# Three of the four weight block sums of each dual of the short convolution's projection by adding transfers, gate loads on SyncE's queue

## The chip, the core and the metric

One core of a Trainium2 chip runs the whole program. The metric is the device time of one execution in microseconds (us); a profile is one further execution taken by the hardware profiler. The engines are TensorE (PE, with weight loads as PEld), VectorE (DVE), ScalarE (ACT), GpSimd (POOL) and SyncE (SP). SP, ACT and POOL also issue DMA transfers, each from a queue of its own that is worked in order.

## What is computed

One layer of a streaming encoder, on 1024 rows of 1024 channels, in float32. The part that matters here is the short convolution's branch of the merge:

```python
h = rms_norm(x, norm_mix_g[l]) * (1.0 + sc1) + sh1
proj = jnp.einsum('bsd,de->bse', h, w_in[l])
b_s, c_s, v_s, v_c, gl_c, gate_br = jnp.split(proj, SPLITS[:-1], axis=-1)
y_a = b_s * causal_dwconv(c_s * v_s, conv_short_w[l])
y_a = jnp.einsum('bsc,cd->bsd', y_a, w_short_out[l])
...
g_a, g_b = jnp.split(jax.nn.sigmoid(gate_br), 2, axis=-1)
mix = jnp.einsum('bsd,de->bse', g_a * y_a + g_b * y_b, w_o[l])
```

The change is in the projection by `w_short_out` and in the loading of `g_a`.

## The kernel before

Channels lie on the 128 partitions and time on the free axis, in two halves of 512 columns. Each float32 operand of a matmul is split into a high part and a low part, so one product of tiles is three matmuls: high by high (line 397), weight high by input low (398), weight low by input high (400). A weight tile of 128 x 1024 is loaded on SP's queue (`load`, line 218), its high part `wh` is cast by ACT (234) and its low part `wl` subtracted by DVE, or by POOL for some (235). `wh` and `wl` have three buffers each; the raw tiles have five, three in one pool and two in another, taken in turn by `raw_tile`.

Most projections are done as duals: two rows of output blocks by a fast scheme of seven block products in place of eight, in the order 1, 2, 6, 5, 7, 3, 4 (`PRODUCTS`). The weights of the products are blocks 11, 12, 21, 22 of the dual or sums of them:

- product 1 uses 11, product 2 uses 12, product 4 uses 22;
- product 5 uses s1 = 21 + 22;
- product 6 uses s2 = 11 + s1;
- product 7 uses 21 + 11;
- product 3 uses 12 + s2.

`apart_units` makes these weights: it loads each block just ahead of its use and adds on the engine it is given. For the short convolution's projection it is called with VectorE for both duals (line 353), so a dual has seven loads (11, 12, 21, 22, 11, 12, 22) and four sums (line 312), of which s2 goes to a tile of its own.

`plan` lists the weights in the order of use, and `next_w` keeps them two products ahead of the matmuls. For this stage the order `ya_order` is product 1 of both duals, product 2 of both, then 6, 5, 7, 3, 4 of dual 0 and the same of dual 1. A product is 24 matmuls. Tile's scheduler lists the instructions of every engine and queue once, at build time, from dependencies and from the orders given with `issue_after`; at run time each engine and queue works its list in order, and waits where an operand or a buffer isn't ready.

`ya_evac` takes the banks of a product. Its `out` (line 1088) loads half of a gate row `ga` (128 x 512, 256 KB) from DRAM on POOL's queue, and DVE multiplies it with the bank into `ma` (lines 747 and 751). Gate tiles share a pool of six buffers with the squares and the statistics of the layer norm, which runs beside this stage: DVE subtracts the mean (1015), ACT squares (1017), DVE sums the squares (1021). The convolved rows `cv` are loaded on SP's queue (1013). Behind the stage follow the other branch's projection (`yb`), whose weights come from `in_w_conf` on the same queue, and on POOL's queue the loads of the other gate (line 1144). Ahead of it POOL subtracts the last low parts of the input projection and adds up `tot` (993).

Of the kernel before, what the change touches and what calls it, by code (L numbers as in the profile page):

```python
# [38 lines left out]
ALU = mybir.AluOpType  # L39
# [76 lines left out]
PRODUCTS = "1265734"  # L116
# [15 lines left out]
def block_kernel(ctx: ExitStack, tc: tile.TileContext, x0, xT, c, vecs, ada, w_first, w_plain, w_duals,  # L132
                 w_short, w_conf, w_o, w_fi, w_fo0, w_fo1, outT):
    nc = tc.nc
# [30 lines left out]
    def ps2_tile(name):  # L165
        return ps2p.tile([P, H], F32, tag="ps2", name=name)
# [4 lines left out]
    def s_tile(name, dt=F32):  # L171
        return hl_tile(name, dt)

    def g_tile(name):
        return gsp.tile([P, H], F32, tag="gs", name=name)

    def f32(t):
        return t.bitcast(F32)

    halves = (slice(0, H), slice(H, T))  # L180
# [28 lines left out]
    def raw_tile(n=1024, home=None):  # L209

        if home is None:
            raws.append(raws.pop(0))
        return (home or raws[-1]).tile([P, 1024], F32, tag="raw", name="raw")[:, :n]

    def load(src, n=1024, home=None):
        raw = raw_tile(n, home)
        with tc.issue_after(x1_load[0]) if x1_load else ExitStack():
            load.ins = nc.sync.dma_start(raw, src).ins
        return raw
# [8 lines left out]
    def split_w(raw, n, after=(), lo_engine=nc.vector):  # L228
        wh = whp.tile([P, 1024], F32R, tag="wh", name="wh")[:, :n]
        wl = wlp.tile([P, 1024], F32R, tag="wl", name="wl")[:, :n]  # L230
        with ExitStack() as order:
            for ins in after:
                order.enter_context(tc.issue_after(ins))
            hi = nc.scalar.copy(wh, raw)  # L234
            lo = lo_engine.tensor_tensor(wl, raw, f32(wh), ALU.subtract)  # L235
        split_w.hi, split_w.lo = hi.ins, lo.ins
        if n == T and lo_engine is nc.gpsimd:
            pool_los.append((hi.ins, lo.ins))
        return wh, wl
# [66 lines left out]
    def apart_units(mats, eng, on_eng=PRODUCTS, after=None):  # L306


        a = {}

        def add(out, x, y):
            unit.eng.tensor_tensor(out, x, y, ALU.add)  # L312
            return out

        def get(b):
            return load(mats[("11", "12", "21", "22").index(b)])

        def unit(m):
            unit.eng = eng if m in on_eng else nc.gpsimd
            if m in "12":  # L320
                raw = get("1" + m)
            elif m == "6":
                for b in ("21", "22", "11"):
                    a[b] = get(b)
                with tc.issue_after(after()) if after else ExitStack():
                    a["s1"] = add(a["22"], a["21"], a["22"])
                    if "6" in on_eng:
                        raw = a["s2"] = add(raw_tile(), a["11"], a["s1"])
                    else:
                        a["s3"] = add(a["21"], a["21"], a["11"])  # L330
                        raw = a["s2"] = add(a["11"], a["11"], a["s1"])
            elif m == "7":
                raw = a["s3"] if "s3" in a else add(a["21"], a["21"], a["11"])
            elif m == "3":
                raw = get("12")
                add(raw, raw, a["s2"])
            else:
                raw = a["s1"] if m == "5" else get("22")
            return split_w(raw, 1024, (), unit.eng)

        return {m: (lambda m=m: unit(m)) for m in PRODUCTS}

    plan = [None] * KC
    plan += [(w_plain[0], 1024)]
    n_duals = len(PAIRS) // 2
# [4 lines left out]
    win_order += [(d, m) for d in range(BEGUN + 1, n_duals) for m in PRODUCTS]  # L350
    plan += [win_units[d][m] for d, m in win_order]
    ya_order = [(d, m) for m in "12" for d in range(2)] + [(d, m) for d in range(2) for m in PRODUCTS[2:]]
    ya_units = [apart_units([w_short[d, m] for m in range(4)], nc.vector) for d in range(2)]
    plan += [ya_units[d][m] for d, m in ya_order]
    plan += [(w[k], 1024) for w in (w_conf, w_o) for ks in (range(KC), SECOND[KEPT:]) for k in ks]
    ready = []
# [212 lines left out]
    gate_dram = {(b, j): dram.tile([P, T], F32, name=f"gate_{b}{j}") for b in "ab" for j in range(KC)}  # L569
# [173 lines left out]
    def plus(out, ps, b):  # L743
        plus.ins = nc.vector.tensor_tensor(out, ps, b, ALU.add).ins
# [150 lines left out]
    b = {}  # L895
# [185 lines left out]
    def ya_evac(d, banks):  # L1081

        st = {}

        def out(i, row, h, op, ps):
            j = 4 * d + 2 * i + row
            ga = g_tile("ga")
            nc.gpsimd.dma_start(ga, gate_dram["a", j][:, halves[h]])
            ma[j, h] = s_tile(f"ma{j}{h}")
            op(ma[j, h], ps, ga)  # L1090
            ma["ins"] = plus.ins

        def evac(i, m, ps):
            if m == "1":
                if d == 1:
                    banks["y", i] = ps2_tile("y")
                nc.scalar.copy(banks["y", i], ps)
            elif m in "65":
                st[m, i] = s_tile("vz")
                nc.scalar.copy(st[m, i], ps)  # L1100
            elif m == "2":
                out(i, 0, 0, times, ps)
            elif m == "7":
                z = ps2_tile("z")
                plus(z, ps, st["5", i])
                out(i, 1, 1, minus_times, z)
            elif m == "3":
                plus(ps, ps, st["6", i])
                out(i, 0, 1, times, ps)
            else:  # L1110
                out(i, 1, 0, minus_times, ps)
        return evac
# [577 lines left out]
```

## Time and profile before

| | us |
|---|---|
| three runs, median (lowest to highest) | 1460.13 (1459.64 to 1461.17) |
| the profiled execution | 1462.66 |
| its span, first to last instruction | 1460.9 |
| PE busy, of the span | 1448.1 |
| DVE busy | 1188.5 |
| ACT busy | 627.2 |
| POOL busy | 516.3 |

The granted TensorE clock was 0.999. A row of a timeline gives the start in us, the busy time in us, the engine, the line of the kernel, the operation, output and inputs by name, and how many instructions were merged; in square brackets stands how long the engine was idle before and what ended it. A row of groups gives count, busy us, mean ns, and the idle time before with its releasers. SPq and POOLq are the queues from which DMA is issued. A PE row's duration overlaps its neighbours, since matmuls are pipelined: the distance of two starts is what one costs.

### The profile page before, as it was taken

The numbers are of one execution on the slowest core, as the hardware profiler recorded it, in microseconds if no ns is written. First come the engines' busy times: TensorE is split into PE (matmuls) and PEld (weight loads), VectorE is DVE, ScalarE is ACT, GpSimd is POOL, SyncE is SP. The second block draws the span as 40 slices with busy tenths as digits, with TensorE's granted clock in tenths as the row PEclk, the third lists the DMA queues.
The fourth block names the chain that finished last, engine by engine and source line by source line (L and its number), as shares of the span: only waits on it lengthen the run. The fifth ranks groups of instructions, "written<-read, shape, count | busy, mean of one in ns | idle before, by whom it ended". The sixth has DMA issues, their size and how long they took to land.

```text
span 1460.9 us, 17711 instructions
## 1 busy us (share of the span) xinstructions
PE 1448.1 (99%) x6394; PEld 1187.8 (81%) x6394; DVE 1188.5 (81%) x1634; ACT 627.2 (43%) x911; POOL 516.3 (35%) x484
## 2 busy tenths in 40 slices
PE   9999999999999999999999999999999999999997
PEld 4878888888888888788888888888888888888887
DVE  7897999987988979999787698777777666866676
ACT  4773333333333346465235465444444443322235
POOL 0007777677677761111021001111111005662505
PEclk9999999999999999999999999999999999999999
DMA  9542222323222357476685436655554449996903
GB/s 351 206 139 85 73 94 79 116 73 101 72 87 73 123 201 281 130 233 206 209 293 203 152 101 216 214 178 198 169 177 148 143 148 327 395 392 193 359 1 116
DMA packets 88522, 257.68 MB, mean 176 GB/s; under 512 B 10177, under 2 KB 12865, under 8 KB 88434
## 3 DMA queue, kind: packets, MB, share of 16 engines
q1 hardware_dynamic: 43792, 142.04, 29.1%
q0 software_dynamic: 40608, 101.92, 21.2%
q10 hardware_dynamic: 4034, 12.59, 2.4%
q8 instruction: 50, 0.82, 0.2%
q14 instruction: 38, 0.31, 0.1%
HBM read 190.97 MB, written 65.54 MB: 176 GB/s over the span
## 4 chain that ended last, share of the span: by engine, by line
PE 88%; issue 4%; DVE 3%; POOL 2%; DMA 1%; ACT 1%; POOLq 0%; DVEq 0%; ACTq 0%
PE bank L400 11%; PE bank L397 11%; PE bank L398 11%; PE x L400 8%; PE x L398 8%; PE x L397 8%; PE z L397 3%; PE z L398 3%; PE z L400 3%; PE mix L400 2%; PE mix L397 2%; PE yb L400 2%; PE yb L397 2%; PE mix L398 2%; PE yb L398 2%
## 5 line engine op out<-in xcount | busy, mean ns | idle before, releaser
L234 ACT CAST wh<-raw 128x1024 fp32r<-128x1024 f32 (+3 forms) x255 | 260.9, 1026 | 475.5 <-PE bank L398 149.5
L235 DVE TENSOR_TENSOR wl<-raw,wh 128x1024 fp32r<-128x1024 f32 (+3 forms) x176 | 209.1, 1190 | 49.3 <-ACT wh L234 46.6
L235 POOL TENSOR_TENSOR wl<-raw,wh 128x1024 fp32r<-128x1024 f32 x79 | 191.4, 2426 | 105.4 <-ACT wh L234 105.3
L972 DVE SCALAR_TENSOR_TENSOR c<-diff,vec,c 128x512 f32<-128x512 f32 x232 | 168.4, 752 | 2.7
L1331 POOL DMA_DIRECT2D hid<-stage x70 | 37.3, 533 | 343.9 <-DVE stage L438 332.5
L400 PE MATMUL bank<-th,wl 128*128 128x512 f32 x312 | 121.5, 389 | 0.4 <-POOL wl L235 0.4
L398 PE MATMUL bank<-tl,wh 128*128 128x512 f32 x312 | 121.4, 389 | 0.0
L397 PE MATMUL bank<-th,wh 128*128 128x512 f32 x312 | 121.4, 389 | 0.0
L972 DVE SCALAR_TENSOR_TENSOR c<-u,wsum,c 128x512 f32<-128x512 f32 x112 | 84.4, 753 | 2.3
L400 PEld LDWEIGHTS bank<-th,wl 128*128 128x128 f32 x312 | 58.6, 188 | 13.0 <-POOL wl L235 0.8
L398 PEld LDWEIGHTS bank<-tl,wh 128*128 128x128 f32 x312 | 58.6, 188 | 12.2
L398 PE MATMUL x<-tl,wh 128*128 128x512 f32 x176 | 68.5, 389 | 0.0
L397 PE MATMUL x<-th,wh 128*128 128x512 f32 x176 | 68.5, 389 | 0.0
L400 PE MATMUL x<-th,wl 128*128 128x512 f32 x176 | 68.4, 390 | 0.0
L397 PEld LDWEIGHTS bank<-th,wh 128*128 128x128 f32 x312 | 58.6, 188 | 12.1
L437 ACT CAST stage<-g 128x512 fp32r<-128x512 f32 x60 | 37.3, 621 | 68.0 <-DMA hid<-stage 42.9
L438 DVE TENSOR_TENSOR stage<-g,stage 128x512 fp32r<-128x512 f32 x60 | 41.3, 690 | 27.2 <-ACT stage L437 27.1
L1355 POOL DMA_DIRECT2D th<-hid x77 | 41.2, 535 | 53.5 <-PE x L400 23.4
L312 POOL TENSOR_TENSOR raw<-raw 128x1024 f32<-128x1024 f32 x8 | 20.5, 2567 | 110.0 <-ACT th L437 104.9
L400 PE MATMUL yb<-zsh,wl 128*128 128x512 f32 x128 | 49.8, 389 | 0.0
L397 PE MATMUL yb<-zsh,wh 128*128 128x512 f32 x128 | 49.8, 389 | 0.0
L398 PE MATMUL yb<-zsl,wh 128*128 128x512 f32 x128 | 49.8, 389 | 0.0
(829 smaller groups left out, 4135.4 us busy)
## 6 DMA issues: line engine op xcount, KB each, us to landing
hid<-stage POOLq DMA_DIRECT2D x70, 512.0 KB, 4.7
raw<-in_w_duals SPq DMA_DIRECT2D x57, 512.0 KB, 3.5
raw<-in_w_fi SPq DMA_DIRECT2D x54, 512.0 KB, 4.7
th<-hid POOLq DMA_DIRECT2D x77, 256.0 KB, 6.0
tl<-hid POOLq DMA_DIRECT2D x77, 256.0 KB, 6.1
ada<-in_ada SPq DMA_DIRECT2D x24, 512.0 KB, 5.7
raw<-in_ada SPq DMA_DIRECT2D x24, 512.0 KB, 4.9
raw<-in_w_fo SPq DMA_DIRECT2D x16, 512.0 KB, 6.1
```

Of the source, the lines that this page charges most:

```text
L234: hi = nc.scalar.copy(wh, raw)
L235: lo = lo_engine.tensor_tensor(wl, raw, f32(wh), ALU.subtract)
L312: unit.eng.tensor_tensor(out, x, y, ALU.add)
L397: nc.tensor.matmul(ps, wh, xh, start=first, stop=False, skip_group_check=again)
L398: nc.tensor.matmul(ps, wh, xl, start=False, stop=False, skip_group_check=again)
L400: mm3.ins = nc.tensor.matmul(ps, wl, xh, start=False, stop=last, skip_group_check=again).ins
L437: t_split.act = nc.scalar.copy(hi, src).ins
L438: t_split.ins = nc.vector.tensor_tensor(lo, src, f32(hi), ALU.subtract).ins
L972: tap.ins = nc.vector.scalar_tensor_tensor(out=out, in0=src[:, s : s + H], scalar=wt, in1=acc, op0=ALU.mult, op1=ALU.add).ins
L1331: nc.gpsimd.dma_start(hid_dram[key], s)
L1355: nc.gpsimd.dma_start(t, hid_dram[key][:, s])
```

## The change

A new function `added_units` makes the weights of the two duals of this stage in place of `apart_units`. Block 22 is loaded and 21 is added onto it by a transfer that adds (s1); 11 is loaded and DVE adds s1 to it (s2); 21 is loaded and 11 is added onto it by a transfer (product 7); 12 is added by a transfer onto s2 in its own tile, once product 6's parts have been split off (product 3). The adding transfers are issued from POOL. Loads are 11, 12, 22, 11, 21, 22 for each dual, adding transfers 21, 11, 12. The second part moves the 16 loads of `ga` halves from POOL's queue to SP's.

```diff
+    def added_units(mats):
+
+
+        a = {}
+        mat = dict(zip(("11", "12", "21", "22"), mats))
+
+        def add(raw, b):
+            nc.gpsimd.dma_start(raw, mat[b], accum_op=ALU.add)
+            return raw
+
+        def unit(m):
+            if m == "6":
+                a["s1"] = add(load(mat["22"]), "21")
+                raw = a["s2"] = load(mat["11"])
+                nc.vector.tensor_tensor(raw, raw, a["s1"], ALU.add)
+            elif m == "7":
+                raw = add(load(mat["21"]), "11")
+            elif m == "3":
+                raw = add(a["s2"], "12")
+            else:
+                raw = a["s1"] if m == "5" else load(mat[{"1": "11", "2": "12", "4": "22"}[m]])
+            return split_w(raw, 1024)
+
+        return {m: (lambda m=m: unit(m)) for m in PRODUCTS}
+
...
-    ya_units = [apart_units([w_short[d, m] for m in range(4)], nc.vector) for d in range(2)]
+    ya_units = [added_units([w_short[d, m] for m in range(4)]) for d in range(2)]
...
-            nc.gpsimd.dma_start(ga, gate_dram["a", j][:, halves[h]])
+            nc.sync.dma_start(ga, gate_dram["a", j][:, halves[h]])
```

## The prediction

> **What bounds the kernel now.** I looked first at the stretches of 20 us, to see where TensorE (PE) is not full, then at PE's instructions in order of time, then at what VectorE (DVE) and ScalarE (ACT) do ahead of the gap. In the stretches the columns are the length, then the busy time and count of PE, its weight loads, DVE, ACT and GpSimd (POOL), the granted clock, and the DMA share and rate.
>
> ```profile
> PE 1448.1 (99%) x6394; PEld 1187.8 (81%) x6394; DVE 1188.5 (81%) x1634; ACT 627.2 (43%) x911; POOL 516.3 (35%) x484
> ...
> 0.00:20.00 20.00, 17.02 (x48) 10.38 (x49) 12.81 (x26) 10.29 (x17) 2.37 (x10) 1.00 0.91 341
> ...
> 600.00:620.00 20.00, 19.45 (x85) 15.45 (x84) 20.00 (x29) 7.00 (x11) 3.04 (x6) 1.00 0.45 141
> ...
> 1440.00:1460.00 20.00, 12.61 (x98) 11.91 (x96) 11.75 (x23) 7.63 (x19) 15.73 (x17) 0.95 0.55 198
> ```
>
> PE is the bound: 12.8 of the span's 1460.9 us are not PE time, 3.0 at the start and 7.4 at the end. The changed stage (about 562 to 643 us) is as full as the rest but for one place, where 85 instructions run in 20 us in place of 90. I number its fourteen products P0 to P13 in the order in which they run: dual 0 and 1 of product 1, dual 0 and 1 of product 2, then 6 5 7 3 4 of dual 0 (P4 to P8) and of dual 1 (P9 to P13).
>
> ```profile
> 607.46 0.39 PE L397 MATMUL bank<-q4h,wh 128*128 128x512 f32 x1
> ...
> 612.68 0.39 PE L400 MATMUL bank<-q4h,wl 128*128 128x512 f32 x1
> 613.09 0.50 PE L397 MATMUL bank<-q6h,wh 128*128 128x512 f32 x1
> ...
> 614.35 0.50 PE L400 MATMUL bank<-q6h,wl 128*128 128x512 f32 x1 [0.53 <-DVE wl L235]
> ...
> 619.51 0.39 PE L397 MATMUL bank<-q5h,wh 128*128 128x512 f32 x1
> ```
>
> P8's 24 matmuls start at 607.46 and the last at 612.68: 5.22 / 23 = 0.227 us each, 5.45 a product. P9 should start at 612.91 and end at 618.36; P10 starts at 619.51. So P9 costs 1.15 us too much, because its low half wl comes late. That is all that the stage has to give.
>
> ```profile
> 593.55 1.31 DVE L747 TENSOR_TENSOR ma<-y,ga 128x512 f32<-128x512 f32 x2 [0.22 <-DMA ga<-gate_a]
> ...
> 595.37 1.22 DVE L235 TENSOR_TENSOR wl<-raw,wh 128x1024 fp32r<-128x1024 f32 x1
> ...
> 597.71 1.22 DVE L312 TENSOR_TENSOR raw<-raw 128x1024 f32<-128x1024 f32 x1
> 598.84 1.29 DVE L1021 TENSOR_TENSOR sq<-sq 128x512 f32<-128x512 f32 x2
> 600.05 1.23 DVE L235 TENSOR_TENSOR wl<-raw,wh 128x1024 fp32r<-128x1024 f32 x1
> ...
> 608.33 1.23 DVE L312 TENSOR_TENSOR raw<-raw 128x1024 f32<-128x1024 f32 x1
> 609.47 1.30 DVE L1021 TENSOR_TENSOR sq<-sq 128x512 f32<-128x512 f32 x2
> 610.67 1.23 DVE L312 TENSOR_TENSOR raw<-raw 128x1024 f32<-128x1024 f32 x1
> 611.80 1.30 DVE L744 TENSOR_TENSOR bank<-bank,vz 128x512 f32<-128x512 f32 x2
> 613.07 1.23 DVE L235 TENSOR_TENSOR wl<-raw,wh 128x1024 fp32r<-128x1024 f32 x1
> ```
>
> Between the last two sums and that subtraction stands ACT's cast, two tiles in one row:
>
> ```profile
> 611.98 2.00 ACT L234 CAST wh<-raw 128x1024 fp32r<-128x1024 f32 x2 [2.83 <-DVE raw L312]
> ```
>
> The chain to the late wl is DVE's own: it works without a break, does P9's two sums at 608.33 (21+22) and 610.67 (with 11), ACT casts at 611.98, DVE subtracts from 613.07 to 614.30, and PE goes on at 614.35.
>
> **The change, part by part.** First the sums taken from DVE.
>
> ```profile
> L312 DVE TENSOR_TENSOR raw<-raw 128x1024 f32<-128x1024 f32 x8 | 9.8, 1223 | 0.6 <-DMA raw<-in_w_short 0.6
> ...
> 622.01 1.22 DVE L312 TENSOR_TENSOR raw<-raw 128x1024 f32<-128x1024 f32 x1
> ...
> 623.74 1.22 DVE L312 TENSOR_TENSOR raw<-raw 128x1024 f32<-128x1024 f32 x1
> ```
>
> Eight sums become two (s2 of each dual). One takes 1.22 us and holds DVE for 1.13 to 1.14 (608.33 to 609.47), so six are 6.8 us of DVE time. Two of them stand between 595 and 611 (597.71, for P7, and 608.33), so P9's remaining sum moves from 610.67 to 608.4, the cast from 611.98 to 609.7 and the subtraction from 613.07 to 610.8, ending at 612.0. That is 0.9 before 612.91: the 1.15 us gap closes. DVE's other relief meets a full PE and is worth nothing.
>
> Second, what replaces them: the raw loads fall from 14 to 12 on SyncE's queue (SP), and POOL issues six adding transfers of 512 KB, each after the load (or, for P7 and P12, after the split of s2) that it adds onto. No adding transfer is in the trace. These rows are nearest: the landing of all raw tiles from 520 to 660 us, and POOL's own transfers.
>
> ```profile
> DMA to landing us min/median/max: 3.4/4.5/8.0
> ...
> hid<-stage POOLq DMA_DIRECT2D x70, 512.0 KB, 4.7
> th<-hid POOLq DMA_DIRECT2D x77, 256.0 KB, 6.0
> ...
> 549.53 3.44 POOL L993 TENSOR_TENSOR tot<-tot,u 128x512 f32<-128x512 f32 x2
> 578.13 0.56 POOL L1088 DMA_DIRECT2D ga<-gate_a  x1 [25.16 <-DVE q7l L913]
> ```
>
> Call its time to landing L. Below, L is a plain load's shortest, 3.4 us; above, an addition that reads its target as well counts as two of the longest, 16.0. I take two medians, 9.0, because the target must be read before it is written. [...]
>
> Whether L is hidden follows from when buffers come free.
>
> ```profile
> 575.50 0.33 SPq L218 DMA_DIRECT2D raw<-in_w_short  x1
> 577.24 0.33 SPq L218 DMA_DIRECT2D raw<-in_w_short  x1
> 587.95 0.33 SPq L218 DMA_DIRECT2D raw<-in_w_short  x1
> 596.66 2.62 SPq L218 DMA_DIRECT2D raw<-in_w_short  x2
> 603.65 0.33 SPq L218 DMA_DIRECT2D raw<-in_w_short  x1
> 617.86 0.33 SPq L218 DMA_DIRECT2D raw<-in_w_conf  x1
> ...
> 626.26 0.79 PE L397 MATMUL bank<-q7h,wh 128*128 128x512 f32 x1
> 632.15 0.39 PE L397 MATMUL bank<-q3h,wh 128*128 128x512 f32 x1
> ```
>
> Five raw buffers turn in a ring, and a dual now takes six tiles where it took eight, so the loads come earlier: dual 1's 22 is the ninth tile, not the twelfth. The ninth now loads at 575.50, into the buffer that the fourth (the same tile in both kernels) leaves, so 22 moves there from 596.66. It lands near 580 and has 21 added by 580 + 0.5 + 9.0 = 589.5; 11 takes the buffer of dual 0's s1, which comes free at 587.95 (the load in that row waits for it now), and lands by 593. P9's sum at 608.4 waits for neither. P11's tile takes the buffer that P7's subtraction frees at 601.3 (600.05 + 1.23): loaded by 605.8, added by 606.3 + L, then 1.05 cast and 1.22 subtraction, due 1.15 before 626.26; that allows L = 16.5. P12's addition waits for the split of s2, which ends by P9's start at 612.9: 613.4 + L + 2.3 must not pass 632.15 - 1.15 = 631.0, so L = 15.3 is the tightest point. At 9.0 every addition is covered, by two products of PE work each. POOL has no work but such issues between 553 and the gate-b loads at 640, so an addition that waits at its head holds nothing else: cost nothing. If L were 20 the cost would be 4.7 us.
>
> Third, the 16 gate loads go to SP, where an issue takes 0.33 us (the rows above) and not the 0.54 of POOL's row below, and where they stand in one line with the weight loads. The last row is SP's waits from 560 to 650 us.
>
> ```profile
> L1088 POOL DMA_DIRECT2D ga<-gate_a x16 | 8.6, 538 | 77.5 <-DVE q7l L913 26.3 <-DVE ma L747 15.6 <-DVE ma L751 10.4
> 588.82 1.13 POOL L1088 DMA_DIRECT2D ga<-gate_a  x2 [8.42 <-DVE ma L747]
> ...
> SPq L218 <- DVE wl L235: 59.2, 12, 13.8
> ```
>
> The issues add 16 x 0.33 = 5.3 us to a queue that mostly waits: loads stand up to 13.8 us for a buffer, 59.2 in all. Such a wait now holds a gate behind it, and a gate's wait for one of six gate buffers holds a weight load. The second is cheap: loads stand ready several us before use (603.65 for a sum at 623.74). The first matters at 588.82, where DVE already waits 0.22 us for the pair to land; P6's subtraction follows at 595.37 to 596.59, just where P6 is due (P8's 607.46 less two products of 5.45: 596.56; its first wl matmul comes 0.45 later). Below, quicker issue gains that 0.22 for DVE and nothing for PE; above, see the second rival. I take nothing, since nearly all releases on both sides are DVE's, in DVE's order, so loads listed by when their buffers come free will not block one another for long.
>
> Sum: -1.15 + 0 + 0. The profiled execution took 1462.66 us, 1.76 outside its span of 1460.9; it becomes 1461.5. It stood 2.53 above the median of the runs, 1460.13, which I take as it is: **1459.0 us**.
>
> **Rivals.** *No net change.* P9's chain shortens but the freed places in DVE's order fill with other work, or a gap of the same size opens at P6 or P11, whose subtractions also end within half a us of their use (596.59; 624.88 is followed by P11 at 626.26). For it: both are due at once on a busy DVE. Against: P11's own two sums, 622.01 and 623.74, go too. Time 1460.1, give or take 0.7.
>
> *A gate waits behind a weight load on SP: slower.* It cannot wait for a DVE instruction that stands behind its own multiplication, or the program would lock; the worst is a load whose buffer the instruction just ahead frees. Then DVE stands for an issue and a landing, 0.33 + about 4.2 (the pair's second issue at 588.82 + 0.57 to its use at 593.55), 4.5 us. Where a subtraction with half a us to spare follows, as P6's does, PE loses 4.0. Without the gain that gives 1464.1, with it 1463.0; it decides once a gate comes over half a us late there. For it: SP's long waits. Against: the order argument above.
>
> *Late additions: slower.* From L = 15.3 on, P12 waits; at L = 20 the time is 1459.0 + 4.7 = 1463.7, at 30 it is 1473.7. For it: nothing like it has been timed, and twice the longest landing, 16.0, is already over. Against: a DMA share of 0.45 from 600 to 620 us, where the last additions fall.
>
> *The order changes further on.* Twelve tiles in place of sixteen shift which of the two raw pools serves each later load, and everything after is listed anew. Later gaps of P9's kind would be 1 us each, either way: 1457.5 to 1463. Against: outside the ends and the gap PE now misses only 12.8 - 3.0 - 7.4 - 0.55 = 1.9 us in all, so few weights can be close to their use.
>
> That the change does nothing at all is excluded: six sums leave DVE.
>
> **How the numbers follow.** Forecast 0.48; no net change 0.18; gate behind a load 0.16; late additions 0.10; later order 0.08 (0.02 faster, 0.03 same, 0.03 slower). About 0.2%, 2.9 us, is what a measurement of this kernel can tell from no change, and the whole gap of the stage is under half of that. So faster 0.02, same 0.48 + 0.18 + 0.03 = 0.69, slower 0.16 + 0.10 + 0.03 = 0.29. The forecast's own range is 1458.0 to 1460.0, for half a us of error in each pitch; the range that holds 8 in 10 runs from 1457.5, the low end of the last rival, to 1464.3, just past one late gate and L = 20.
>
> **What would show it.** P9 follows P8 without a break, with its subtraction ended before its first wl matmul; two sums by DVE in the stage, 6.8 us less; adding transfers that land in 3.4 to 16 us, with no ACT cast or DVE sum idle for them; no DVE idle of over half a us for a gate; SP's waits with no gate stuck. A PE wait for wl or wh at P6, P11 or P12 would make the forecast wrong, and its releaser says which rival it was.

## The result, and the profile after

| | before | after |
|---|---|---|
| median of seven runs (lowest to highest), us | 1460.86 (1459.64 to 1462.97) | 1466.25 (1463.57 to 1467.48) |
| the profiled execution, us | 1462.66 | 1463.58 |
| its span, us | 1460.9 | 1461.8 |

The changed kernel is slower: after over before is 1.0028, 95% interval 1.0019 to 1.0038, or 5.4 us. The two profiled executions differ by only 0.9 us, since the one of before lies above its median and the one of after is one of its fastest runs. So the traces are to be read for what happens, and the medians for how much.

First the page of the changed kernel:

```profile
PE 1447.1 (99%) x6394; PEld 1187.6 (81%) x6394; DVE 1178.1 (81%) x1628; ACT 629.0 (43%) x911; POOL 512.2 (35%) x474
```

PE's work is the same, but 14.7 us of the span are not PE time, where it was 12.8. Next the changed stage in its timeline: DVE's sum for P9 (line 357 now, s2 of dual 1), ACT's cast and DVE's subtraction for P9, and PE at the end of P8 (q4) and the start of P9 (q6).

```profile
605.54 1.22 DVE L357 TENSOR_TENSOR raw<-raw 128x1024 f32<-128x1024 f32 x1
606.85 2.00 ACT L234 CAST wh<-raw 128x1024 fp32r<-128x1024 f32 x2 [0.49 <-DVE raw L357]
...
607.93 1.22 DVE L235 TENSOR_TENSOR wl<-raw,wh 128x1024 fp32r<-128x1024 f32 x1
...
612.47 0.39 PE L425 MATMUL bank<-q4h,wl 128*128 128x512 f32 x1
612.69 0.39 PE L422 MATMUL bank<-q6h,wh 128*128 128x512 f32 x1
```

The wl of P9 ends at 607.93 + 1.22 = 609.15, 3.5 us before P9, and P9 follows P8 one pitch later: the gap of 1.15 us is closed. The adding transfers, from the views of the source line 350:

```profile
L350 POOL DMA_DIRECT2D raw<-in_w_short x6: 862/865/908, 554.3 to 609.5; - x6
...
DMA to landing us min/median/max: 5.5/7.2/8.6
```

They land in 5.5 to 8.6 us, and in that view no instruction waits for one. So the stage did what it should, and the loss is elsewhere. The one new break in PE's timeline lies 300 us later, in the feed-forward's input projection (weights `in_w_fi`). It is in the second half of product 5 of its dual 2 (output bank `z`). First after, then before; lines of after are 25 higher than before's from the new function on.

```profile
912.64 0.39 PE L425 MATMUL z<-t5h,wl 128*128 128x512 f32 x1
...
915.49 0.50 PE L422 MATMUL z<-t5h,wh 128*128 128x512 f32 x1 [2.46 <-DVE g L1321]
```

```profile
914.03 0.39 PE L400 MATMUL z<-t5h,wl 128*128 128x512 f32 x1
...
914.63 0.51 PE L397 MATMUL z<-t5h,wh 128*128 128x512 f32 x1 [0.22 <-DVE g L1296]
```

Take off one pitch of 0.227 us, and PE loses 915.49 - 912.64 - 0.23 = 2.62 us where it lost 0.37. It waits for DVE to empty a bank of product 2 (`g<-y`, line 1321, before 1296), into which the second half of product 5 goes. With the gap at P9 closed that is 2.25 - 1.15 = +1.1 us for the traced pair, of which 0.9 was measured. What DVE waits for is seen in the same timeline of after on the other engines (SPq: loads of weights; POOL: stores of the activations from the three `stage` buffers; ACT and DVE fill these):

```profile
903.96 2.67 SPq L218 DMA_DIRECT2D raw<-in_w_fi  x2
...
905.65 0.53 POOL L1356 DMA_DIRECT2D hid<-stage  x1 [7.83 <-ACT stage L462]
...
907.47 0.53 POOL L1356 DMA_DIRECT2D hid<-stage  x1 [1.29 <-DVE g L1365]
...
910.88 0.62 ACT L462 CAST stage<-g 128x512 fp32r<-128x512 f32 x1 [1.50 <-DMA hid<-stage]
911.53 0.69 DVE L463 TENSOR_TENSOR stage<-g,stage 128x512 fp32r<-128x512 f32 x1 [1.05 <-ACT stage L462]
...
913.49 0.62 ACT L462 CAST stage<-g 128x512 fp32r<-128x512 f32 x1 [1.98 <-DMA hid<-stage]
...
914.14 0.69 DVE L463 TENSOR_TENSOR stage<-g,stage 128x512 fp32r<-128x512 f32 x1 [1.91 <-ACT stage L462]
914.75 0.68 DVE L1321 TENSOR_TENSOR g<-y,g 128x512 f32<-128x512 f32 x1
```

Read it from the end. The `g<-y` of 914.75 was not held up itself: it stands in DVE's list behind the stage subtraction of 914.14, which waited 1.91 us for ACT's cast of 913.49, which waited 1.98 us for a store to leave a stage buffer. Before:

```profile
907.79 0.53 POOL L1331 DMA_DIRECT2D hid<-stage  x1 [7.84 <-ACT stage L437]
909.31 0.53 POOL L1331 DMA_DIRECT2D hid<-stage  x1 [0.99 <-DVE stage L438]
...
911.42 0.62 ACT L437 CAST stage<-g 128x512 fp32r<-128x512 f32 x1
912.63 0.62 ACT L437 CAST stage<-g 128x512 fp32r<-128x512 f32 x1 [0.59 <-DVE stage L438]
...
915.78 0.33 SPq L218 DMA_DIRECT2D raw<-in_w_fi  x1
```

There the same two casts found their buffers free. The landing times of the two stores that decide, first before, then after:

```profile
DMA to landing us min/median/max: 2.9/3.1/3.2
```

```profile
DMA to landing us min/median/max: 5.2/5.5/5.9
```

The stores took nearly twice as long. Beside them ran two weight loads that come some 11 us earlier than before, at 903.96 and 906.30 instead of from 915.78 on. From 905 to 910 us the DMA share is 0.97 after and 0.25 before; a part of this difference is that before's two stores start 2 us later.

Why do loads of a stage 300 us later move? The five raw buffers are taken in turn from a list of two pools. The stage took 16 raw tiles (14 loads and two tiles for s2) and now takes 12, so every later load finds the list at another place: 16 leaves it one place on from where it was, 12 two. SP's list of weight loads after the stage is then another one. Before, and after:

```profile
649.90 2.07 SPq L218 DMA_DIRECT2D raw<-in_ada  x2
653.44 2.14 SPq L218 DMA_DIRECT2D raw<-in_w_conf  x2
```

```profile
648.52 0.33 SPq L218 DMA_DIRECT2D raw<-in_ada  x1
650.26 0.33 SPq L218 DMA_DIRECT2D raw<-in_w_conf  x1
```

### The profile page after: what moved, and what is told of

The parts are those of the page before. It is cut to its first block, busy times and chain, and to the rows that moved or that the text cites. A ratio compares the mean times of both kernels' runs of the same rounds, so it can differ in the third digit from the quotient of the medians.

```text
span 1461.8 us, 17723 instructions
## 1 busy us (share of the span) xinstructions
PE 1447.1 (99%) x6394; PEld 1187.6 (81%) x6394; DVE 1178.1 (81%) x1628; ACT 629.0 (43%) x911; POOL 512.2 (35%) x474
## 4 chain that ended last, share of the span: by engine, by line
PE 93%; POOL 2%; DMA 1%; DVE 1%; ACT 1%; issue 1%; POOLq 0%; ACTq 0%; DVEq 0%
PE bank L425 12%; PE bank L422 12%; PE bank L423 12%; PE x L425 8%; PE x L422 8%; PE x L423 8%; PE z L422 3%; PE z L423 3%; PE z L425 3%; PE y L422 2%; PE y L425 2%; PE y L423 2%; PE mix L425 2%; PE mix L423 2%; PE yb L425 2%; PE yb L423 2%
```

## Experiments

The theory: the place of the ring moves two loads of the feed-forward ahead, these slow the stores, and PE waits at the z bank. Rivals: the adding transfers or the gate loads themselves cost the time, or the freed gap is lost again nearby. There were three batches, each with runs of the kernel before beside it on the same chip; the medians of before were 1461.03, 1461.50 and 1461.16 us.

**The ring put back.** The changed kernel, with the list of pools turned four places once the stage's last tile is taken, so that it stands where before's does (12 + 4 = 16):

```diff
+    def turn(n, unit):
+        w = unit()
+        for _ in range(n):
+            raws.append(raws.pop(0))
+        return w
+
     plan += [ya_units[d][m] for d, m in ya_order]
+    plan[-1] = lambda u=plan[-1]: turn(4, u)
```

> The changed kernel with one thing added: after the stage's last weight tile the list of raw pools is turned by four places, so that every later load gets the pool (of the three-buffer or the two-buffer one) that it had in the kernel before. Theory A (the changed kernel lost its time in the feed-forward stage near 912 us, because twelve raw tiles in place of sixteen turned the ring by one place and so moved later weight loads against the hid stores): the 2.5 us wait of PE for the z bank near 912 falls below 0.6 us, P9's gap stays closed, time 1459.0 to 1460.0. Theory B (the gates on SyncE's queue did it): the wait stays, 1463.5 to 1467.5. Theory C (the work just comes 1.4 us earlier and so meets the stores at a worse time, whatever the ring): the wait stays, 1463.5 to 1467.5.

Measured: 1461.72 us (1460.38 to 1464.02), 1.0006 [0.9998, 1.0015]. The order of SP's loads is before's again, and the two loads are back behind the stores:

```profile
647.68 2.07 SPq L218 DMA_DIRECT2D raw<-in_ada  x2
651.22 2.14 SPq L218 DMA_DIRECT2D raw<-in_w_conf  x2
...
913.43 1.42 SPq L218 DMA_DIRECT2D raw<-in_w_fi  x2
```

The wait at the z bank is down to 0.24 us and P9 still follows P8 without a break. The loss is gone; but the time is level with before's, not below it as expected.

**The ring alone.** The kernel before, nothing changed but the list turned by one place behind the stage (16 + 1 leaves the place that 12 leaves):

```diff
+    plan[-1] = lambda u=plan[-1]: turn(1, u)
```

> The kernel before with one thing added: after the stage's last weight tile the list of raw pools is turned by one place, to the position that it has in the changed kernel. Sums on DVE and gates on POOL's queue as before. Theory A: P9's gap of 1.15 us stays and the wait for the z bank in the feed-forward stage appears, 1463 to 1468. Theories B and C: nothing of the change is in it, and nothing comes earlier: 1460.9 give or take 1.

Measured: 1465.31 us (1464.81 to 1466.81), 1.0029 [1.0018, 1.0040].

```profile
905.74 2.67 SPq L218 DMA_DIRECT2D raw<-in_w_fi  x2
...
914.10 0.39 PE L409 MATMUL z<-t5h,wl 128*128 128x512 f32 x1
...
917.24 0.66 PE L406 MATMUL z<-t5h,wh 128*128 128x512 f32 x1 [2.75 <-DVE g L1305]
```

This kernel has no adding transfer and its gates are on POOL, and its median loses 4.28 us: 2.91 us go at the z bank, and the matmuls behind it come 0.43 us apart for a while (granted clock 0.50 from 917.5 to 920.5 us), which is taken up below. The place of the ring alone is enough for a loss of this size. In its trace the loss is all in one place: from PE's first matmul in the feed-forward (818.01 us in before's first trace) to its first behind that product 5 (917.53) it takes 103.6 us, where before's two traces take 99.5 and 99.0.

**The adding transfers alone.** The gate loads go back to POOL's queue:

```diff
-            nc.sync.dma_start(ga, gate_dram["a", j][:, halves[h]])
+            nc.gpsimd.dma_start(ga, gate_dram["a", j][:, halves[h]])
```

> The adding transfers alone; the gate halves stay on POOL's queue. Theory A: as the changed kernel, 1463.5 to 1467.5, with the wait for the z bank and without P9's gap. Theory B: 1459.0 to 1460.0, without the wait. Theory C: as theory A.

Measured: 1468.84 us (1462.55 to 1471.07), 1.0046 [1.0030, 1.0061], the slowest of all and above what was expected. Beside the wait at the z bank (3.23 us here) PE has new ones in the stage, as its waits show (us in total, times, longest):

```profile
PE z L422 <- DVE g L1321: 3.1, 1, 3.1
PE bank L425 <- DVE wl L235: 1.9, 1, 1.9
...
PE bank L422 <- DVE ma L772: 1.1, 1, 1.1
```

Its timeline on POOL and DVE shows where they start:

```profile
583.30 0.86 POOL L350 DMA_DIRECT2D raw<-in_w_short  x1 [6.21 <-DMA raw<-in_w_short]
583.84 1.45 POOL L1113 DMA_DIRECT2D ga<-gate_a  x2
...
590.38 0.69 DVE L772 TENSOR_TENSOR ma<-bank,ga 128x512 f32<-128x512 f32 x1 [5.48 <-DMA ga<-gate_a]
```

An adding transfer waits 6.21 us at the head of POOL's queue for the load that it adds onto, the first gate pair stands behind it until 583.84, and DVE then stands 5.48 us for the gate. So the two parts of the change belong together.

**The gates alone.** The kernel before with the gate loads on SP's queue:

```diff
-            nc.gpsimd.dma_start(ga, gate_dram["a", j][:, halves[h]])
+            nc.sync.dma_start(ga, gate_dram["a", j][:, halves[h]])
```

> The gate halves on SyncE's queue alone; the block sums stay on DVE, so sixteen raw tiles are taken. Theory A: as the kernel before, 1460.9 give or take 1, P9's gap open, the wait for the z bank under 0.6 us. Theory B: 1463.5 to 1467.5 with the wait. Theory C: as the kernel before. A gate stuck behind a weight load would show as DVE idle for DMA ga of over half a us.

Measured: 1461.47 us (1459.97 to 1462.31), 1.0001 [0.9993, 1.0010]; P9's gap is there as before, and there is no wait at the z bank. The gates on SP cost nothing by themselves.

**Two of the early loads held.** The ring could act in other ways than by these loads. So in the changed kernel the first two loads of the feed-forward's dual 3 were held behind the emptying of the z bank: DVE writes one column of the raw tile at that point, and the load has to follow it.

```diff
     def load(...):
...
+        if held:
+            with tc.issue_after(held.pop()):
+                nc.vector.memset(raw[:, :1], 0.0)
...
+                in_evac.y = nc.vector.tensor_tensor(ha[f, "1"], ps, ha[f, "1"], ALU.add).ins
+                if (d, p) == (2, 1):
+                    in_evac.y_2 = in_evac.y
...
+        if (d, m) == (3, "1"):
+            held.extend([in_evac.y_2] * 2)
```

> The changed kernel with two one-column writes added on DVE: the first two weight loads of dual 3 in the feed-forward stage (those that started at 903.96 and 906.30 us there, and at 915.78 and later in the kernel before) can't start before DVE has done the second y bank of dual 2. Nothing else moves in any queue. Theory A, in its closer form (the ring let these two loads start 12 us earlier, they share the DMA engines with the hid stores, the stores land in 5 to 6 us in place of 3, ACT and DVE wait for the stage buffers, and PE for the y bank): stores from 905 to 913 land in under 4 us, PE's wait for the z bank is under 0.6 us, time 1459.4 to 1460.4, below the kernel before. Rival (the stores are late for another reason, or the order itself is at fault): the wait of 2 us or more stays, 1463.5 to 1467.5.

Measured: 1462.50 us (1461.06 to 1463.78), 1.0005 [0.9996, 1.0014]; the z wait is 1.85 us. The timeline shows that the edit missed its aim:

```profile
903.42 12.89 SPq L221 DMA_DIRECT2D raw<-in_w_fi  x3
```

Other loads of the same dual took the places of the held ones, two of them at 903.42 and 905.76. It settles little.

**The change again.** The changed kernel, unedited, on another chip.

> The changed kernel once more, for a second trace and more times. Its first seven runs fell in two groups, three at 1463.6 to 1464.5 with a granted clock of 0.998 to 0.999 and four at 1466.3 to 1467.5 with 0.996 to 0.997. Theory D: when PE's wait for the z bank is longer than some 2.7 us the granted clock falls for several us, and that costs 2 us more. Then a trace with a wait of 2.7 us or more shows matmul starts 0.43 us apart behind it and a span near 1464.5, one with less shows 0.23 and a span near 1462. Without D the span is the wait plus 1459.3 in both.

Measured: 1465.85 us (1464.06 to 1467.88), 1.0029 [1.0016, 1.0041].

```profile
913.88 0.39 PE L425 MATMUL z<-t5h,wl 128*128 128x512 f32 x1
916.43 0.53 PE L422 MATMUL z<-t5h,wh 128*128 128x512 f32 x1 [2.16 <-DVE g L1321]
...
917.18 0.63 PE L425 MATMUL z<-t5h,wl 128*128 128x512 f32 x1
917.61 0.63 PE L422 MATMUL z<-t5h,wh 128*128 128x512 f32 x1
```

The wait is shorter than in the first trace, 2.32 us, and yet the run is 2.9 us longer. Behind the wait eight matmuls come 0.41 to 0.43 us apart instead of 0.227. In the stretch from 916 to 920 us the granted clock is 0.60:

```profile
916.00:920.00 4.00, 3.57 (x9) 2.85 (x10) 3.85 (x5) 2.50 (x5) 0.99 (x2) 0.60 0.82 251
```

The twelve matmuls of this half take 4.45 us (916.43 to 920.88), in the first trace of after 2.85 (915.49 to 918.34): 1.6 us more. That is a second price of the same wait. The 2.7 us of the expectation is not a threshold: here the clock fell behind a shorter wait.

The longer half and the shorter wait together make 1.3 of the 2.9 us. Another 0.8 us lies in the changed stage, at P6 (product 7 of dual 0, `q7`):

```profile
594.82 1.31 DVE L772 TENSOR_TENSOR ma<-y,ga 128x512 f32<-128x512 f32 x2 [2.50 <-DMA ga<-gate_a]
...
596.64 1.22 DVE L235 TENSOR_TENSOR wl<-raw,wh 128x1024 fp32r<-128x1024 f32 x1
...
596.91 0.39 PE L423 MATMUL bank<-q7l,wh 128*128 128x512 f32 x1
...
597.91 0.50 PE L425 MATMUL bank<-q7h,wl 128*128 128x512 f32 x1 [0.62 <-DVE wl L235]
```

DVE stands 2.50 us for a pair of gate halves, so P6's subtraction starts at 596.64, where the first trace has it at 593.56, and PE loses 597.91 - 596.91 - 0.23 = 0.77 us. SP issued the pair about 1 us later than in the first trace (587.53, there 586.48), and its halves landed 7.2 us after their issue, there 3.7 and 5.2. The trace of the kernel with two loads held has the same (DVE 2.05 us, PE 0.52), and the other six traces of kernels with both parts of the change don't. What made the pair late in these two is not shown.

**The ring put back again**, the first experiment's kernel beside it.

> The kernel with the ring turned back once more, since its profiled run (span 1458.6) was the fastest of eleven and the median 1461.72, above the 1459.0 to 1460.0 that theory A gave. If what remains is a smaller wait for the z bank that varies from run to run, a trace with a span near 1460 shows that wait at 1 to 2 us; if it is elsewhere, PE's waits name another place.

Measured: 1461.38 us (1460.10 to 1462.07), 0.9998 [0.9989, 1.0006]. Loads from 913.85, 0.48 us at the z bank, no break at P9. The mechanism stands, and again there is no gain.

**The ring turned two places** in the changed kernel, a place that neither kernel has.

> The changed kernel with the list of raw pools turned by two places behind the stage, a position that neither kernel has. Theory A says that the time goes with the position: it may lie anywhere from 1459.4 (the later loads clear of the hid stores) to 1468, and what it is must again be read from the wait for the z bank and the weight loads that start between 900 and 913 us: loads there, a wait of over 2 us; none there, a wait under 0.6.

Measured: 1461.43 us (1460.29 to 1463.48), 0.9999 [0.9990, 1.0008]. One load goes early, at 903.29, the next at 913.33; no wait at the z bank.

**All four loads held.** As the fifth, with `* 4` in the place of `* 2`, so that no load of that dual can pass.

> As the run that held two loads, but with all four loads of dual 3 held behind the second y bank of dual 2. There, the queue passed the two held loads by, and the other two of the four went out at 903.42 and 905.76 us, so the hid stores still had company: the wait fell only to 1.85 us. Theory A in its closer form: with no weight load between 900 and 913 us the stores from 905 to 913 land in under 4 us, ACT waits under 1 us in all for the stage buffers there, PE's wait for the z bank is under 0.6 us, time 1460.5 to 1461.5, level with the kernel whose ring was turned back. Rival (the stores are late for another reason): the wait stays at 1.8 us or more, time 1462 or above.

Measured: 1461.97 us (1460.80 to 1464.06), 1.0007 [0.9999, 1.0016]. Its loads, and then the longest of PE's waits in the feed-forward:

```profile
911.92 3.47 SPq L221 DMA_DIRECT2D raw<-in_w_fi  x5
```

```profile
PE x L426 <- DVE g L1333: 0.6, 1, 0.6
PE x L426 <- ACT g L1325: 0.5, 1, 0.5
```

The ring stands where the change leaves it, the loads start at 911.92, the two stores land in 2.9 and 3.6 us, and the wait at the z bank is gone. So it is the early loads, and not the ring in another way, that make the wait. The held loads come late for two places further on, 0.6 and 0.5 us.

**The kernel before again**, for the spread.

> The kernel before once more, for a second trace. Its first trace, 1462.66 us, was slower than all but one of its later runs. Theory A: P9's gap of 1.1 to 1.2 us is there again, the wait for the z bank is under 0.6 us, and from the 148 us mark to the last gap near 1430 it takes about 1282.6 us, where the kernels with the ring turned back or by two took 1281.0 to 1281.6. If the second trace takes 1281.5 or less, the gain of P9's gap is not there in most runs of the kernel before, and that is why the ring-corrected kernels are only level with it.

Measured: 1460.72 us (1459.73 to 1462.32), 0.9999 [0.9990, 1.0008]; the traced run, 1462.32, has P9's gap and no wait at the z bank. Between the two marks of the expectation it takes 1282.4 us (148.09 to 1430.49), as in the first trace, so the gap costs its time here too.

**The ring turned three places**, to test the rule that two loads between 903 and 908 us make the wait, and one or none doesn't.

> The changed kernel with the list of raw pools turned by three places behind the stage, the one position besides one more that no run has had. The rule from the runs so far: two weight loads started between 903 and 908 us give a wait of 1.8 us or more for the z bank, one at 903.3 or none gives 0.5 or less. So this kernel is at 1460.5 to 1461.7 with at most one such load, and at 1463 to 1468 with two.

Measured: 1464.98 us (1462.44 to 1466.84), 1.0025 [1.0014, 1.0036].

```profile
904.19 2.67 SPq L218 DMA_DIRECT2D raw<-in_w_fi  x2
...
912.64 0.39 PE L434 MATMUL z<-t5h,wl 128*128 128x512 f32 x1
...
915.67 0.79 PE L431 MATMUL z<-t5h,wh 128*128 128x512 f32 x1 [2.65 <-DVE g L1330]
```

Two loads early, a wait of 2.80 us and the lower clock behind it, 0.50 from 916 to 920 us. Four of the ring's five places have now been seen: two with the early pair (slower by 0.25 to 0.3%), two without (level).

The landing of the two deciding stores orders all thirteen traces. In the six with two loads beside them they land in 5.2 to 6.2 us, and PE loses 1.85 to 3.23 us at the z bank; in the seven with one such load or none they land in 2.9 to 3.6 us, and PE loses 0 to 0.48. The DMA share from 905 to 910 us doesn't order them: it is 0.65 in the ring alone, where PE waits, and 0.81 with the ring turned two places, where it doesn't.

## Why the prediction was wrong, point by point

**The stage.** Right in the first trace. P9's subtraction was put at 610.8 and ran at 607.93, the gap closed, two sums stay on DVE. The time to landing was taken as 9.0 us with bounds of 3.4 and 16.0; it is 7.2, and the limit of 15.3 was not near. The 9.0 and the 16.0 were estimates of the author, each two landings of a plain load, on the argument that an addition reads its target first; no run shows that reading, only the six landings of 5.5 to 8.6 us. The rival of late additions falls. The rival "No net change" does not: it named P6 as a place where a new gap could open, and in two of the eight traces with both parts of the change one did, of 0.77 and 0.52 us.

**The gates on SP.** Right at nothing for the gates alone, which are level with before. With the adding transfers beside them it is not always nothing: in the same two traces DVE stood 2.50 and 2.05 us for a gate, far over the half us that the prediction gave as the sign, and P6's gap came of it. The rival put 4.0 us of PE's time on this; it was 0.77 and 0.52. The traces don't separate its cause, the place behind a weight load, from the slower landing.

**"An addition that waits at its head holds nothing else".** Right for the change as a whole, but by its second part: with the gates left on POOL, the same waits cost PE 1.9 + 1.1 us in the stage. The prediction priced the two parts one by one and so did not see that one protects the other.

**The failed step** is the rival "The order changes further on". It named the cause, "Twelve tiles in place of sixteen shift which of the two raw pools serves each later load", and gave it 0.08 and "1 us each, either way". The argument against it was that PE missed only 1.9 us elsewhere, "so few weights can be close to their use". That asked only whether a load comes late. What hurt was a load that came early: beside it and a second one the stores that hold the stage buffers landed in 5.2 and 5.9 us, where before's landed in 2.9 and 3.2 without them, and through ACT's and DVE's order that held back a PSUM bank, by 2.62 us. Before, that bank came 0.37 us late in one trace and just in time in the other, and the prediction shows no such row. The size was off too: the wait is 2.3 to 2.9 us in place of 1, and behind it the granted clock fell to 0.50 in four of the six traces that have the wait.

**The sum by the runs.** 2.25 more at the z bank, less 1.15 at P9, is +1.1 us without the lower clock; with it (1.6 us in the trace of the repeat, at least 2.4 in that of the ring turned three places: 5.29 us for twelve matmuls) it is 2.7 to 3.5. P6's gap can add 0.8. The median's 5.4 us remains larger than this, though the interval begins at 2.8 (0.19% of 1460.86), and in the repeat it was 4.35. Of the 7.25 us between the forecast of 1459.0 and the measured 1466.25, 0.73 is the base: the prediction took 1460.13, the median of three of the seven runs of before.

The seven runs of after divide by their mean clock: three at 0.998 and 0.999 take 1463.57 to 1464.46, four at 0.996 and 0.997 take 1466.25 to 1467.48. The traced run is one of the three. The kernel with the ring turned three places divides in the same way, two runs at 0.999 (1462.44 and 1462.47) and five at 0.996 and 0.997 (1464.88 to 1466.84). The kernel with two loads held waits 1.85 us, has no run below 0.998, and its median is only 1.0 us above before's. That points to the lower clock, and not the wait itself, as the larger part of the loss. That the clock made the difference in the four slower runs of the change is argued from their clock figures, as none of them was traced.

**Half open: the gain of 1.15 us.** In the traces it is there. From PE's break at 148 us (its end is at 149.05 in before's first trace) to the first matmul of `mix` (773.59), the four traces without adding transfers take 624.5 to 625.0 us. Of the eight with both parts of the change six take 623.4 us, and the two with P6's gap 624.3 and 624.0. In the medians it isn't seen: the kernels without the wait at the z bank, with the ring turned four or two places, take 1461.72, 1461.38 and 1461.43, against 1461.03 and 1461.50 of before in the same batches. For the first of these the interval begins at 0.9998 and leaves no room for 1.15 us, which is 0.08%; for the other two it does. The traces must not be taken for the medians: before's two traced runs are slow ones of their kernel (1462.66 and 1462.32), the three with the ring turned are faster than their medians (1460.38, 1460.82, 1460.45), and PE's break at 148 us, ahead of all that was edited, ends between 147.7 and 149.1. A gap at P6 in the runs that were not traced would be one way for the gain to be lost; no run shows it. No kernel here beats before by a difference that can be measured.

## What to carry to other kernels

When a change alters how many tiles a stage takes from a shared ring, everything behind it is loaded in another order, at once and for the rest of the program: compare the order of the loads, or restore the ring's place, before judging the change by its time. Look for what is late by little or just in time (here a bank, 0.37 us late in one trace and not in another), and ask which transfers run beside the stores behind it; a load that comes earlier need not be free: beside two that came some 11 us early the stores landed in 5.5 us, where it was 3.1. And before a transfer that waits for another goes to a queue, see what else stands in that queue: here gates behind adding transfers cost 3.0 us of PE's waits, and the transfers had 1.15 us to save. One trace is not enough to call a gap closed or a wait absent: the second trace of this kernel had a wait at P6 that the first had not.

## What the hardware showed that was not expected

**Behind a wait of 2.32 us the granted clock fell to 0.50, and behind one of 2.62 it stayed at 1.00.** Behind waits of 2.32, 2.80, 2.91 and 3.23 us the matmuls ran 0.43 us apart at a granted clock of 0.50, for eight in the first case (from 917.0 to 920.0 us); behind 1.85 and 2.62 us they ran 0.23 us apart, at 1.00. Length alone does not order these, and what else does is not shown.

**An adding transfer's issue** holds POOL for 0.865 us, where the stores of 512 KB above take 0.53; its landing, at 7.2 us, is longer than the 5.1 that is the median of the seven plain loads of `in_w_short` from 550 to 645 us in the same trace (3.9 for the fourteen before).
